# Conformer/RG-LRU block on one core: squares of the opening norm shared by two engines, and a gate operation moved ahead of convolution taps

## The chip, the cores and the metric

One core of a Trainium2 chip runs the whole program. The metric is the device time of one execution in microseconds (us); the kernel before took 876.96 us (median of 3 runs, 875.38 to 878.05). The core has five engines that work side by side and wait for each other through semaphores: TensorE (PE in the profile, its weight loads PEld), VectorE (DVE), ScalarE (ACT), GpSimd (POOL) and SyncE (SP), whose queue issues the DMAs here. [...]

## The reference, cut to what matters

One layer over 512 latent tokens and 256 context tokens, 1024 channels, all in fp32.

```python
hl = modulate(rmsnorm(x, g_pre_mix), sh1, sc1)        # sh, sc from silu(c) @ w_ada + b_ada
hc = modulate(rmsnorm(ctx, g_pre_mix), csh1, csc1)
glu, xr, gt, mg = split(hl @ w_in)                    # the context needs xr alone
u   = dwconv31(v * sigmoid(g))                        # Conformer branch, then LayerNorm, silu, projection
xr  = dwconv4(xr) + b
for d in (forward, backward):
    r = sigmoid(xr @ w_r[d] + b_r[d]);  i = sigmoid(xr @ w_i[d] + b_i[d])
    a = exp(-8 * r * softplus(-lam[d]));  u = sqrt(1 - a*a) * i * xr
    h_t = a_t * h_(t-1) + u_t                         # scan; the latents start from the context's last state
y  = (sigmoid(ga) * yA + sigmoid(gb) * ((sum of h) * gelu(gt)) @ w_lru) @ w_out
x  = x + gt1 * rmsnorm(y)
x  = x + gt2 * rmsnorm(conv_ffn(modulate(rmsnorm(x)), 3x3))
```

## The kernel before, in words

Activations lie with channels on the 128 partitions (8 blocks `b` of 128 channels) and tokens along the free dimension. Every matrix product is made of three fp32r matmuls (L134 to L136): a value is split into a high part (ACT copies it to fp32r) and a low part (a subtraction). For weights that is the pair L122 (ACT, `whi`) and L123 (`wlo`, mostly POOL, for some blocks DVE), called ahead of their use by `cvt_to`; for activations it is `split` (L138 to L140). So PE needs ACT and POOL behind every 128x1024 block of weights.

**The beginning** (L349 to L439). The four 128-token blocks of `x` are loaded; `norm_a` squares each on ACT with a running sum (L227), takes the root on ACT (L149), its reciprocal (L151) and the scaling (L230) on DVE. `norm_b` transposes the scaled blocks on PE and copies them out, half on DVE and half on ACT (L239, L241). Meanwhile `ada_mm(0)` makes the first shift and scale columns. `ada_h(q)` then modulates two channel blocks (`h`, L293, on DVE) and splits them into `Ahi` and `Alo`. The first matmuls of the program's main products (`firsts`, L378) wait for these.

**The loop over channel blocks** (L667 to L731, `b` = 1 to 8) does four things at a time: PE makes `xr`, `v`, `g`, `gt` products of blocks ahead and the four gate products of block b-1 (`gate_mm`); ACT does tanh, exp and the roots; DVE does the width-4 convolution (`xr_post`, L569 to L576), the gate operations `r_dve` (L613), `i_dve` (L617), the product `scans_mul` (L630, its second direction on POOL) and the scans of block b-2 (L636 to L638). PSUM gives the products of `xr` and of the gates two 1024-wide buffers in turn, so the next `xr` product must wait until `r_dve(b-1, 1)` has read its gate.

**The taps.** The width-31 depthwise convolution (`conv31`, L505) is a generator of DVE instructions: 244 of them, two blocks at a time, called taps here. `fill(n)` places the next n taps at that point of DVE's program. In the loop before, iterations 1 to 7 place 4 + 4 + 2 + 3 + 3 = 16 taps and iteration 8 places 8 + 6 + 3 + 3 = 20, 132 in all. The other 112 follow behind the loop (L775 to L790), beside the products `gb` and `yb`, 15 for each block. When they are done, POOL adds up the last blocks (`lnsum`, L533) and PE makes the LayerNorm's mean (`mean`, L814).

**Between loop and taps** DVE multiplies by the gelu branch and splits (`gt_post`, L660 and L140, tile `rgl`). ACT's `ga_act` (L763) reuses memory and waits for the last of these; behind it on ACT stand two tap products handed to ACT and POOL (`offload`, L545, L547), the gates `tg` and weight conversions, behind those on POOL the conversions `wlo` of the next weights.

The order of the work is written out by hand: there is no scheduler.

Of the kernel before, what the change touches and what calls it, by code (L numbers as in the profile page):

```python
# [8 lines left out]
F32 = mybir.dt.float32  # L9
F32R = mybir.dt.float32r  # L10
AF = mybir.ActivationFunctionType
ALU = mybir.AluOpType
PSUM = bass.MemoryType.PSUM

D = 1024
NB = 8
T = 512
TC = 256
TA = T + TC
# [4 lines left out]
EPS = 1e-6  # L24
# [13 lines left out]
def backbone_kernel(es: ExitStack, tc: tile.TileContext, x, ctxt, par, wadq, wada, win, wgate, wpc, wpl, wout,  # L38
                    wup, wdn, out):
    nc = tc.nc  # L40
    V, S, G, PE = nc.vector, nc.scalar, nc.gpsimd, nc.tensor
# [5 lines left out]
    st = es.enter_context(tc.tile_pool(name="st", bufs=4))  # L47
# [17 lines left out]
    ones = const.tile([128, 128], F32, name="ones")  # L65
# [3 lines left out]
    def flat(t):  # L69
        return t.rearrange("p a b -> p (a b)") if len(t.shape) == 3 else t  # L70

    def mm2(name):
        return ps_mm.tile([128, 1024], F32, tag="mm2", name=name)
# [88 lines left out]
    xs = pg.tile([128, 4, D], F32, tag="g", name="xs")  # L162
    xnT = pd.tile([128, NB, T], F32, tag="d", name="xnT")
    Ahi = pa.tile([128, NB, T], F32R, name="Ahi")
    Alo = pa.tile([128, NB, T], F32R, name="Alo")
# [57 lines left out]
    def norm_a(src_rows, slot, junk):  # L223
        if src_rows is not None:
            nc.sync.dma_start(out=slot, in_=src_rows)
        ss = st.tile([128, 1], F32, tag="ss", name="ss")
        S.activation(out=junk, in_=slot if len(junk.shape) == 2 else slot.rearrange("p (a b) -> p a b", b=junk.shape[2]),  # L227
                     func=AF.Square, accum_out=ss)
        r = rstd_of(ss, "x")
        V.tensor_scalar(out=slot, in0=slot, scalar1=r, scalar2=None, op0=ALU.mult)  # L230
# [14 lines left out]
    for v, nm in ((0, "c"), (1, "c_ctx")):  # L245
        S.activation(out=sT[:, :, v:v + 1], in_=col(nm).unsqueeze(2), func=AF.Silu)


    adl = const.tile([128, 48], F32, name="adl")
    adc = const.tile([128, 16], F32, name="adc")  # L250
    ggb = const.tile([128, D], F32, name="ggb")
    gsl = const.tile([128, 8], F32, name="gsl")
# [3 lines left out]
    def ada_load(q):  # L256
        for k2 in range(4):
            wq[q, k2] = pq.tile([128, 2, 512], F32, tag="wa", bufs=10, name="wa")
            nc.sync.dma_start(out=wq[q, k2], in_=wadq[q, :, 2 * k2:2 * k2 + 2, :])
# [19 lines left out]
    def ada_h(q):  # L279
        big, R = adp[q]  # L280
        tp = big[:, 128:256]
        PE.transpose(tp, R[:, 0:128], idn)
        tv = tp.rearrange("p (m j v) -> p m j v", m=2, j=2)
        for v, dst, gs in ((0, adl, gsl), (1, adc, gsc)):
            V.tensor_add(dst[:, 0:16].rearrange("p (m b) -> p m b", m=2)[:, :, 2 * q:2 * q + 2], tv[:, :, :, v],
                         col("b_ada", 0, 16).rearrange("p (m b) -> p m b", m=2)[:, :, 2 * q:2 * q + 2])
            V.scalar_tensor_tensor(out=gs[:, 2 * q:2 * q + 2], in0=dst[:, 8 + 2 * q:10 + 2 * q], scalar=1.0,
                                   in1=col("g_pre_mix", 2 * q, 2), op0=ALU.add, op1=ALU.mult)
            if v == 0:
                hs = []  # L290
                for k in (2 * q, 2 * q + 1):
                    h = t_tile("h")
                    V.tensor_scalar(out=h, in0=xnT[:, k, :], scalar1=gsl[:, k:k + 1], scalar2=adl[:, k:k + 1],  # L293
                                    op0=ALU.mult, op1=ALU.add)
                    hs.append(h)
                for k, h in zip((2 * q, 2 * q + 1), hs):
                    split(h, Ahi[:, k, :], Alo[:, k, :])
# [46 lines left out]
    def warm(ps, n):  # L344
        for _ in range(n):
            PE.matmul(ps[:, 0:128], ones, ones, start=True, stop=True)

    psA, psC = mm2("xr_ps"), mm2("vg_ps")
    for t in range(4):  # L349
        norm_a(x[128 * t:128 * t + 128, :], xs[:, t, :], flat(Alo[:, 2 * t:2 * t + 2, :]))  # L350
    ada_load(0)
    warm(psA, 20)
    for t in range(4):
        norm_b(xs[:, t, :], xnT[:, :, 128 * t:128 * t + 128])
# [87 lines left out]
    pre = st.tile([128, 1], F32, tag="sd", name="pre")  # L442
# [107 lines left out]
    rec = pd.tile([128, NB, T], F32, tag="d", name="rec")  # L550
    filler = conv31()

    def fill(n):
        for _ in range(n):
            if not next(filler, False):
                return
# [75 lines left out]
    def scans(b):  # L632
        (a0, _), (a1, _) = lru[b, 0], lru[b, 1]
        u0, u1 = lru[b, 0, 1], lru[b, 1, 1]
        hc = pl.tile([128, TC], F32, tag="hc", name="hc")
        V.tensor_tensor_scan(hc, a0[:, T:TA], u0[:, T:TA], 0.0, ALU.mult, ALU.add)  # L636
        V.tensor_tensor_scan(rec[:, b, :], a0[:, 0:T], u0[:, 0:T], hc[:, TC - 1:TC], ALU.mult, ALU.add)  # L637
        V.tensor_tensor_scan(u1[:, TA - 1::-1], a1[:, TA - 1::-1], u1[:, TA - 1::-1], 0.0, ALU.mult, ALU.add)  # L638
        (V if b == 7 else G).tensor_add(rec[:, b, :], rec[:, b, :], u1[:, 0:T])

# [26 lines left out]
    for b in range(1, NB + 1):  # L667
        last = b == NB
        if last:
            gt_block(3)  # L670
            gt_copy(3)
        else:
            w = W(("xr", b))
            if b == 1:
                ps = ps1
            else:
                ps = mm2("xr_ps")
                block(ps[:, 0:T], w, Ahi, Alo)
        if b >= 2:
            scans_act(b - 2)  # L680
        if not last:
            block(ps[:, T:T + TP], w, chi, clo)
        fill(8 if last else 4)
        if b >= 2:
            scans_mul(b - 2)
        W(("gate", b - 1))
        gate_mm(b - 1, 0, 0)
        if not last:
            xw = xr_act(b, ps)
        r_act(b - 1, 0)  # L690
        if b + 1 < NB:
            psv = mm1("v_ps")
            block(psv, W(("v", b + 1)), Ahi, Alo)
        else:
            gt_block(1 if b < NB else 4)
            gt_copy(1 if b < NB else 4)
        fill(0 if last else 4)
        if not last:
            xr_post(b, ps, xw, 0)
            xc_new = xcs.pop(b)  # L700
        r_dve(b - 1, 0)
        if b >= 2:
            scans(b - 2)
        fill(6 if last else 2)
        gate_mm(b - 1, 0, 1)
        if last:
            gt_block(5)
        gate_mm(b - 1, 1, 0)
        gate_tanh(b - 1, 0, 1)
        r_act(b - 1, 1)  # L710
        i_dve(b - 1, 0)
        if b + 1 < NB:
            glu_mul(tg, psv, b + 1)
        if b + 2 < NB:
            psg = mm1("g_ps")
            block(psg, W(("g", b + 2)), Ahi, Alo)
        else:
            gt_block((0, 2, 6)[b - 6])
            if not last:
                gt_copy((0, 2)[b - 6])  # L720
        fill(3)
        r_dve(b - 1, 1)
        fill(3)
        gate_mm(b - 1, 1, 1)
        gate_tanh(b - 1, 1, 1)
        if not last:
            xcs[b] = xc_new
            xc_split(b)
        if b + 2 < NB:
            tg = gate_act(psg)  # L730
        i_dve(b - 1, 1)  # L731
# [509 lines left out]
```

## Time and profile before

| what | value |
|---|---|
| median of 3 runs | 876.96 us (875.38 to 878.05) |
| the profiled execution's own time | 875.37 us |
| its span in the trace | 873.6 us |
| PE busy | 851.4 us (97%) |
| DVE busy | 662.5 us (76%) |
| ACT busy | 432.5 us (50%) |
| POOL busy | 410.7 us (47%) |
| mean granted TensorE clock | 0.996 |

The span is what the trace's times count; 1.8 us of the execution lie around it. "Busy" is a mean over stages: the strip of 40 slices on the page shows PE at 7 tenths in the first slice and 9 in all others but the last, and DVE at 3 to 5 tenths in the first four, at 9 from the sixth to the seventeenth, and at 3 to 5 for some slices after the eighteenth. A matmul's record is longer than its share of the engine, because matmuls overlap: a 128x512 one is 0.39 us long and the next starts 0.23 us after it.

### The profile page before, as it was taken

What the parts mean: (1) busy time and instruction counts of PE and PEld (TensorE: products, weight loads), DVE (VectorE), ACT (ScalarE), POOL (GpSimd) and SP (SyncE); (2) the same over time, 40 slices, a digit from 0 to 9 for tenths busy, and PEclk for the clock granted to TensorE, in tenths of its full rate; (3) what the DMA queues carried; (4) which work ended last, traced back from release to release, by engine and by line L of the source; (5) the groups of instructions that cost most, each with busy time, mean ns of one, the idle gap of its engine ahead of it and who ended that gap; (6) DMA issues with size and microseconds to landing.
All of it is one profiled execution on the core that took longest, in us unless ns stands there. A gap on an engine that the chain in (4) does not pass through costs nothing.

```text
span 873.6 us, 11376 instructions
## 1 busy us (share of the span) xinstructions
PE 851.4 (97%) x4312; PEld 690.1 (79%) x4312; DVE 662.5 (76%) x929; ACT 432.5 (50%) x614; POOL 410.7 (47%) x227
## 2 busy tenths in 40 slices
PE   7999999999999999999999999999999999999997
PEld 6777877887787878887688889888888888888785
DVE  4355899999998999973555254999998998989204
ACT  5283776686767542225743355544443444345222
POOL 1234554555555665464232313545655456457720
PEclk9999999999999999999999999999999999999999
DMA  9952122121222232252843411224333333324402
GB/s 352 385 210 85 62 83 75 66 79 61 85 73 96 73 111 83 97 192 95 339 145 121 179 39 50 97 96 136 118 121 108 121 120 107 115 94 134 156 0 97
DMA packets 31398, 106.01 MB, mean 121 GB/s; under 512 B 3440, under 2 KB 3568, under 8 KB 31344
## 3 DMA queue, kind: packets, MB, share of 16 engines
q1 hardware_dynamic: 31344, 105.29, 34.4%
q8 instruction: 34, 0.56, 0.3%
q14 instruction: 20, 0.16, 0.1%
HBM read 103.17 MB, written 2.10 MB: 121 GB/s over the span
## 4 chain that ended last, share of the span: by engine, by line
PE 79%; DVE 11%; ACT 5%; issue 3%; DMA 0%; POOL 0%; DVEq 0%; SPq 0%; ACTq 0%; POOLq 0%
PE up_ps L135 9%; PE up_ps L136 9%; PE up_ps L134 9%; PE xr_ps L134 3%; DVE rec L637 3%; PE xr_ps L135 3%; PE xr_ps L136 2%; DVE cv L521 2%; PE ya_ps L134 2%; PE y_ps L135 2%; PE ya_ps L136 2%; PE y_ps L134 2%; PE ya_ps L135 2%; PE y_ps L136 2%; PE yb_ps L134 1%
## 5 line engine op out<-in xcount | busy, mean ns | idle before, releaser
L123 POOL TENSOR_TENSOR wlo<-raw,whi 128x1024 fp32r<-128x1024 f32 x117 | 291.8, 2507 | 232.9 <-ACT whi L122 232.7
L1035 DVE SCALAR_TENSOR_TENSOR cv<-zall,P,cv 128x512 f32<-128x512 f32 x240 | 161.8, 743 | 0.2
L521 DVE SCALAR_TENSOR_TENSOR cv<-glu,P,cv 128x512 f32<-128x512 f32 x228 | 153.8, 740 | 0.0
L122 ACT ACTIVATE whi<-raw 128x1024 fp32r<-128x1024 f32 x121 | 125.2, 1053 | 22.5 <-issue 8.0
L134 PE MATMUL up_ps<-Ahi,whi 128*128 128x512 f32 (+1 forms) x352 | 131.8, 375 | 0.0
L136 PE MATMUL up_ps<-Ahi,wlo 128*128 128x512 f32 (+1 forms) x352 | 131.7, 374 | 0.0
L135 PE MATMUL up_ps<-Alo,whi 128*128 128x512 f32 (+1 forms) x352 | 131.6, 374 | 0.0
L135 PEld LDWEIGHTS up_ps<-Alo,whi 128*128 128x128 f32 x352 | 66.0, 188 | 13.2
L136 PEld LDWEIGHTS up_ps<-Ahi,wlo 128*128 128x128 f32 x352 | 66.0, 188 | 13.3
L134 PEld LDWEIGHTS up_ps<-Ahi,whi 128*128 128x128 f32 x352 | 66.0, 188 | 13.1
L1021 POOL TENSOR_TENSOR acl<-fo,ach 128x512 fp32r<-128x512 f32 x20 | 26.0, 1300 | 85.5 <-ACT ach L1018 85.5
L1035 DVE SCALAR_TENSOR_TENSOR cv<-zall,P,cc 128x512 f32<-128x512 f32 x40 | 43.2, 1108 | 21.2 <-ACT cc L1009 21.2
L1007 ACT ACTIVATE zall<-up_ps 128x512 f32<-128x512 f32 x40 | 23.7, 593 | 63.5 <-PE up_ps L136 63.5
L1018 ACT ACTIVATE ach<-fo 128x512 fp32r<-128x512 f32 x20 | 12.7, 633 | 66.8 <-DVE fo L1017 66.8
L598 ACT ACTIVATE gate_ps<-gate_ps,P 128x768 f32<-128x768 f32 x32 | 28.0, 875 | 34.2 <-PE gate_ps L136 33.7
L134 PE MATMUL xr_ps<-Ahi,whi 128*128 128x512 f32 x56 | 22.6, 404 | 6.9 <-DVE e L613 6.9
L364 ACT ACTIVATE tg<-gb_ps 128x512 f32<-128x512 f32 x8 | 4.8, 596 | 48.9 <-PE gb_ps L136 48.9
L1009 ACT ACTIVATE cc<-up_ps,P 128x512 f32<-128x512 f32 x40 | 27.3, 682 | 1.9 <-DVE cv L1035 1.9
L1035 DVE SCALAR_TENSOR_TENSOR fo<-zall,P,cv 128x512 f32<-128x512 f32 x40 | 27.9, 734 | 0.0
L140 POOL TENSOR_TENSOR xl<-xc,xh 128x768 fp32r<-128x768 f32 x8 | 14.9, 1859 | 27.5 <-ACT xh L139 27.5
L134 PE MATMUL gt_ps<-Ahi,whi 128*128 128x512 f32 x64 | 26.0, 407 | 1.5 <-DVE e L613 1.5
L136 PE MATMUL gt_ps<-Ahi,wlo 128*128 128x512 f32 x64 | 25.9, 404 | 0.3 <-POOL wlo L123 0.3
(380 smaller groups left out, 2120.9 us busy)
## 6 DMA issues: line engine op xcount, KB each, us to landing
raw<-in_win_dram SPq DMA_DIRECT2D x48, 512.0 KB, 3.3
raw<-in_wup_dram SPq DMA_DIRECT2D x40, 512.0 KB, 3.3
wa<-in_wada_dram SPq DMA_DIRECT2D x24, 512.0 KB, 5.7
raw<-in_wdn_dram SPq DMA_DIRECT2D x22, 512.0 KB, 3.4
wa<-in_wadq_dram SPq DMA_DIRECT2D x16, 512.0 KB, 9.1
raw<-in_wpl_dram SPq DMA_DIRECT2D x8, 512.0 KB, 3.3
raw<-in_wpc_dram SPq DMA_DIRECT2D x8, 512.0 KB, 4.8
raw<-in_wout_dram SPq DMA_DIRECT2D x8, 512.0 KB, 3.3
```

The source lines that it names most:

```text
L122: S.activation(out=flat(hl[0]), in_=flat(t), func=AF.Copy)
L123: eng.tensor_sub(flat(hl[1]), flat(t), flat(hl[0]))
L134: PE.matmul(o, lh, rh, start=first, stop=False)
L135: PE.matmul(o, lh, rl, start=False, stop=False)
L136: PE.matmul(o, ll, rh, start=False, stop=last)
L521: V.scalar_tensor_tensor(out=cv[b] if k else glu[:, b, 0:T], in0=glu[:, b, k:k + T], scalar=col("dw31", 31 * b + k, 1), in1=cv[b], op0=ALU ...
L598: S.activation(out=lru[b, d, q], in_=lru[b, d, q], func=AF.Tanh, scale=0.5, bias=hb[:, i:i + 1])
L637: V.tensor_tensor_scan(rec[:, b, :], a0[:, 0:T], u0[:, 0:T], hc[:, TC - 1:TC], ALU.mult, ALU.add)
L1007: S.activation(out=z[:, 1:1 + GH, 1:1 + GW], in_=ps.rearrange("p (r c) -> p r c", c=GW), func=AF.Copy)
L1009: S.activation(out=c, in_=ps.rearrange("p (r c) -> p r c", c=GW), func=AF.Copy, scale=col("dw9", 9 * (i + FW * (1 - s)) + 4, 1))
L1021: G.tensor_sub(acl[:, i, :], fo[i, 0], ach[:, i, :])
L1035: V.scalar_tensor_tensor(out=o, in0=zz[i, s][:, k // 3:k // 3 + GH, k % 3:k % 3 + GW], scalar=col("dw9", 9 * (i + FW * (1 - s)) + k, 1), i ...
```

## The change

- Beginning: ACT squares blocks 0 and 2 of `x`, DVE (as a product of the block with itself, with a running sum) blocks 1 and 3. The root's function table is loaded by a one-column root (`pre`) ahead of the first square. Sums and roots lie in two tiles of four columns.
- `ada_h(0)`: the first of its two modulated blocks is made by ACT (`Identity` with scale and bias), the second by DVE as before.
- Loop: `r_dve(b-1, 1)` stands ahead of the taps that stood before it. The taps of iterations 2 to 7 fall from 16 to 14, those of iteration 8 from 20 to 19; iteration 1 keeps 16. That makes 119 taps in the loop and 125 behind it.
- Scans: the context's scan writes over its input `u0` instead of a tile `hc`, and the latents' scan starts from that column.

```diff
@@ before the start
+    pre = st.tile([128, 1], F32, tag="sd", name="pre")
+    S.activation(out=pre, in_=ones[:, 0:1], func=AF.Sqrt)
@@ ada_h
-                    V.tensor_scalar(out=h, in0=xnT[:, k, :], scalar1=gsl[:, k:k + 1], scalar2=adl[:, k:k + 1],
-                                    op0=ALU.mult, op1=ALU.add)
+                    if k:
+                        V.tensor_scalar(out=h, in0=xnT[:, k, :], scalar1=gsl[:, k:k + 1], scalar2=adl[:, k:k + 1],
+                                        op0=ALU.mult, op1=ALU.add)
+                    else:
+                        S.activation(out=h, in_=xnT[:, k, :], func=AF.Identity, scale=gsl[:, k:k + 1],
+                                     bias=adl[:, k:k + 1])
@@ the opening norm
+    ss4, sd4 = [st.tile([128, 4], F32, tag="n4" + n, bufs=1, name="n4" + n) for n in "sd"]
     for t in range(4):
-        norm_a(x[128 * t:128 * t + 128, :], xs[:, t, :], flat(Alo[:, 2 * t:2 * t + 2, :]))
+        nc.sync.dma_start(out=xs[:, t, :], in_=x[128 * t:128 * t + 128, :])
     ada_load(0)
+    for t in (1, 0, 3, 2):
+        junk = flat(Alo[:, 2 * t:2 * t + 2, :])
+        if t % 2:
+            V.scalar_tensor_tensor(out=junk, in0=xs[:, t, :], scalar=1.0, in1=xs[:, t, :], op0=ALU.mult, op1=ALU.mult,
+                                   accum_out=ss4[:, t:t + 1])
+            continue
+        S.activation(out=junk, in_=xs[:, t, :], func=AF.Square, accum_out=ss4[:, t:t + 1])
+        for i in (t, t + 1):
+            S.activation(out=sd4[:, i:i + 1], in_=ss4[:, i:i + 1], func=AF.Sqrt, scale=1.0 / D, bias=EPS)
+            V.reciprocal(sd4[:, i:i + 1], sd4[:, i:i + 1])
+            V.tensor_scalar(out=xs[:, i, :], in0=xs[:, i, :], scalar1=sd4[:, i:i + 1], scalar2=None, op0=ALU.mult)
@@ scans
-        hc = pl.tile([128, TC], F32, tag="hc", name="hc")
-        V.tensor_tensor_scan(hc, a0[:, T:TA], u0[:, T:TA], 0.0, ALU.mult, ALU.add)
-        V.tensor_tensor_scan(rec[:, b, :], a0[:, 0:T], u0[:, 0:T], hc[:, TC - 1:TC], ALU.mult, ALU.add)
+        V.tensor_tensor_scan(u0[:, T:TA], a0[:, T:TA], u0[:, T:TA], 0.0, ALU.mult, ALU.add)
+        V.tensor_tensor_scan(rec[:, b, :], a0[:, 0:T], u0[:, 0:T], u0[:, TA - 1:TA], ALU.mult, ALU.add)
@@ the loop over b
-        fill(0 if last else 4)
+        fill(0 if last else 4 if b == 1 else 3)
...
-        fill(3)
         r_dve(b - 1, 1)
-        fill(3)
+        fill(6 if b == 1 else 5)
```

The loop on DVE, iteration 2, from the context's scan to `i_dve(1, 1)`; `e` is the decay factor that `r_dve` works on, `cv` and `glu` are the taps' tiles, `u` is `i_dve`'s result. Before:

```order
L636 SCALAR_TENSOR_TENSOR hc<-a,u 128x256
L637 SCALAR_TENSOR_TENSOR rec<-a,hc,u 128x512
L638 SCALAR_TENSOR_TENSOR u<-a,u 128x768
...
L368 SCALAR_TENSOR_TENSOR glu<-tg,v_ps 128x512
L521 SCALAR_TENSOR_TENSOR cv_921<-glu,P,cv_921 128x512
L521 SCALAR_TENSOR_TENSOR cv_923<-glu,P,cv_923 128x512
L521 SCALAR_TENSOR_TENSOR cv_921<-glu,P,cv_921 128x512
L613 SCALAR_TENSOR_TENSOR e_1221<-e_1221,gate_ps 128x768
```

And now:

```order
L655 SCALAR_TENSOR_TENSOR u<-a,u 128x256
L656 SCALAR_TENSOR_TENSOR rec<-a,u 128x512
L657 SCALAR_TENSOR_TENSOR u<-a,u 128x768
...
L388 SCALAR_TENSOR_TENSOR glu<-tg,v_ps 128x512
L633 SCALAR_TENSOR_TENSOR e_1211<-e_1211,gate_ps 128x768
L541 SCALAR_TENSOR_TENSOR cv_915<-glu,P,cv_915 128x512
L541 SCALAR_TENSOR_TENSOR cv_913<-glu,P,cv_913 128x512
L541 SCALAR_TENSOR_TENSOR cv_915<-glu,P,cv_915 128x512
```

The gate operation (L613, now L633) stands directly behind the `glu` product, and five taps follow it before `i_dve` where three stood ahead and three behind.

DVE at the beginning, from its first instruction to the copies of the transposed blocks; `n4s` and `n4d` are the sums and roots. Before:

```order
L151 RECIPROCAL rsx<-sdx 128x1
L230 TENSOR_SCALAR xs<-xs,rsx 128x1024
...
L241 COPY xnT<-tp_ps 128x4x128 x4
L277 COPY R<-ada_ps 128x128
L285 TENSOR_TENSOR adl<-ada_ps,P 128x2x2
L287 SCALAR_TENSOR_TENSOR gsl<-adl,P 128x2
L293 TENSOR_SCALAR h<-xnT,gsl,adl 128x512 x2
L140 TENSOR_TENSOR Alo<-h,Ahi 128x512 x2
```

And now:

```order
L364 SCALAR_TENSOR_TENSOR Alo,n4s<-xs 128x1024
L370 RECIPROCAL n4d<-n4d 128x1
L371 TENSOR_SCALAR xs<-xs,n4d 128x1024
...
L241 COPY xnT<-tp_ps 128x4x128 x4
L280 COPY R<-ada_ps 128x128
L288 TENSOR_TENSOR adl<-ada_ps,P 128x2x2
L290 SCALAR_TENSOR_TENSOR gsl<-adl,P 128x2
L297 TENSOR_SCALAR h<-xnT,gsl,adl 128x512
L140 TENSOR_TENSOR Alo<-h,Ahi 128x512 x2
```

DVE has two squares more ahead of the copies (the second stands in the rows left out, between the second and the third scaling) and one modulation less.

## Rows read from the trace of the kernel before

**Rows 1.** Waits of PE, 110 to 260 us and 260 to 320: total, times, longest.
```profile
PE xr_ps L134 <- DVE e L613: 6.9, 5, 1.4
...
PE gt_ps L134 <- DVE e L613: 1.5, 1, 1.5
```

**Rows 2.** Windows: length, busy us of each engine, granted clock, DMA share, GB/s.
```profile
134.30:159.90 25.60, 24.23 (x122) 20.16 (x122) 25.25 (x30) 18.71 (x23) 13.89 (x7) 1.00 0.22 73
...
280.00:282.00 2.00, 1.93 (x5) 1.54 (x6) 2.00 (x5) 1.99 (x3) 0.00 (x0) 0.55 0.71 221
282.00:284.00 2.00, 2.00 (x7) 1.57 (x6) 2.00 (x4) 1.98 (x3) 0.60 (x1) 0.60 0.11 43
```

**Rows 3.** Timeline of DVE in one loop iteration: start us, length us, instruction.
```profile
147.02 2.06 DVE L521 SCALAR_TENSOR_TENSOR cv<-glu,P,cv 128x512 f32<-128x512 f32 x3
149.00 0.94 DVE L613 SCALAR_TENSOR_TENSOR e<-e,gate_ps 128x768 f32<-128x768 f32 x1
...
155.33 2.02 DVE L630 TENSOR_TENSOR u<-u,e 128x768 f32<-128x768 f32 x1
```

**Rows 4.** Timeline of PE in the same iteration.
```profile
148.34 0.28 PE L136 MATMUL gate_ps<-xh,gwl 128*128 128x256 f32 x1
149.99 0.50 PE L134 MATMUL xr_ps<-Ahi,whi 128*128 128x512 f32 x1 [1.37 <-DVE e L613]
```

**Rows 5.** Timeline of POOL in the same iteration.
```profile
154.69 1.85 POOL L630 TENSOR_TENSOR u<-u,e 128x768 f32<-128x768 f32 x1
```

**Rows 6.** The chain of waits, 296 to 320 us: start us, length us, piece.
```profile
314.48 1.50 POOL wlo L123
...
316.03 0.50 PE gb_ps L136
```

**Rows 7.** Timeline of DVE: the first taps behind the loop.
```profile
307.86 13.25 DVE L521 SCALAR_TENSOR_TENSOR cv<-glu,P,cv 128x512 f32<-128x512 f32 x20
```

**Rows 8.** Timeline of POOL: the last sums for the mean.
```profile
385.36 2.47 POOL L533 TENSOR_TENSOR lnsum<-lnsum,glu 128x512 f32<-128x512 f32 x2 [1.47 <-DVE glu L521]
```

**Rows 9.** Timeline of PE: the mean.
```profile
396.82 1.02 PE L814 MATMUL mean<-lnsum,ones 128*128 128x512 f32 x2
```

**Rows 10.** The scans' lines: count, shortest/median/longest ns, first and last start.
```profile
L637 DVE TENSOR_TENSOR_SCAN rec<-a,hc,u x8: 3232/3235/3248, 113.9 to 285.2; 128x512 f32<-128x512 f32 x8
...
L638 DVE TENSOR_TENSOR_SCAN u<-a,u x8: 1725/1726/1727, 117.1 to 288.4; 128x768 f32<-128x768 f32 x8
```

**Rows 11.** Timeline of ACT at the beginning.
```profile
4.84 1.06 ACT L227 ACTIVATE Alo<-xs 128x1024 fp32r<-128x1024 f32 x1 [0.45 <-DMA xs<-in_x_dram]
5.80 0.19 ACT L227 ACTIVATION_READ_ACCUMULATOR Alo<-xs 128x1 f32 x1
6.00 1.28 ACT L149 ACT_TABLE_LOAD   x1
7.30 0.20 ACT L149 ACTIVATE sdx<-ss 128x1 f32<-128x1 f32 x1
```

**Rows 12.** Timeline of SP: weight loads that wait for blocks 0 and 1 of x.
```profile
5.22 1.21 SPq L105 DMA_DIRECT2D raw<-in_win_dram  x2
```

**Rows 13.** Timeline of DVE at the beginning.
```profile
11.35 0.17 DVE L151 RECIPROCAL rsx<-sdx 128x1 f32<-128x1 f32 x1 [0.32 <-ACT sdx L149]
11.55 0.76 DVE L230 TENSOR_SCALAR xs<-xs,rsx 128x1024 f32<-128x1024 f32 x1
...
18.56 3.00 DVE L293 TENSOR_SCALAR h<-xnT,gsl,adl 128x512 f32<-128x512 f32 x2
21.80 1.29 DVE L140 TENSOR_TENSOR Alo<-h,Ahi 128x512 fp32r<-128x512 f32 x2 [0.24 <-ACT Ahi L139]
```

**Rows 14.** Timeline of POOL at the beginning.
```profile
18.48 2.35 POOL L123 TENSOR_TENSOR w0l<-raw,w0h 128x1024 fp32r<-128x1024 f32 x1 [1.26 <-ACT w0h L122]
```

**Rows 15.** Groups by line and form of DVE and of ACT: busy us, mean ns.
```profile
L931 DVE SCALAR_TENSOR_TENSOR x<-xw,rsy,x 128x1024 f32<-128x1024 f32 x4 | 5.1, 1285 | 0.1
...
L857 ACT ACTIVATE glu<-glu,P 128x512 f32<-128x512 f32 x8 | 6.4, 805 | 1.9 <-DVE glu L856 1.9
```

## The prediction, made before the run

> **What bounds the kernel now.** I read the table of busy shares first: PE is busy 97% of the span, so little is to be had except where PE stands still, and a change off PE's path counts only through PE's waits. So the second view is PE's waits by releaser. From 110 to 260 us one line holds all of them: five waits of the `xr` product on DVE's gate operation, 6.9 us together, the longest 1.4; behind 260 us the same operation holds `gt` up once, for 1.5 us [rows 1]. The third view is the windows: one iteration of the loop, 25.60 us, has PE busy 24.23 and DVE busy 25.25 [rows 2]. There DVE is the bound, and PE loses the difference, 1.37 us. The fourth is the timeline of one iteration. DVE works off three taps from 147.02, then the gate operation from 149.00 for 0.94 [rows 3]; PE's last gate matmul starts at 148.34 and the next product only at 149.99, behind a wait of 1.37 [rows 4]. A tap costs (149.00 - 147.02) / 3 = 0.66 us; the record of the three ends at 149.08, so DVE's instructions overlap by 0.08.
>
> **The change, part by part.**
>
> *Gate operation ahead of the taps.* It needs nothing from them. It would start at 147.02 and end at 147.96. PE's last gate matmul starts at 148.34 and lasts 0.28, so PE itself is ready at about 148.5: 0.5 us later. The wait goes, in iterations 2 to 6.
>
> *Two taps fewer per iteration.* Reordering alone would only move the wait, since DVE's work per iteration (25.25) exceeds PE's (24.23). Less 2 x 0.66 it is 23.93, and PE is the bound, by 0.3 us. What is late next is DVE's multiplication L630: it starts at 155.33 and takes 2.02 [rows 3], because POOL's own half runs from 154.69 to 156.54 [rows 5]; it ends about 0.8 us behind POOL's end, however early it starts. With one tap ahead of it gone the gain there is lost, and only the tap behind it shortens the way to the next gate operation. By my count this uses up nearly all of the 0.5 us. I take 6.8 of the 6.9 us; the bounds are 3.4 (half of each wait stays) and 6.9.
>
> *Behind the loop.* Iteration 8 has one tap less between its gate operation and the end of `gt_post`: DVE is there 0.66 earlier. [...] But the chain of waits shows what is next: POOL's `wlo` at 314.48 releases PE's `gb` at 316.03 [rows 6]. That chain hangs on DVE: `gt_post` ends as the taps begin at 307.86 [rows 7], ACT and POOL follow. [...] Only 0.66 is kept. A wait longer than the one of 1.5 probably costs the clock again: I take 1.6 us back; bounds 0 and 1.7.
>
> *125 taps behind the loop for 112.* From 307.86, 20 taps take 13.25 [rows 7], 0.66 each; 13 more are 8.6 us. POOL's last sums ended at 385.36 + 2.47 = 387.83 [rows 8], the mean started at 396.82 [rows 9]: 9.0 us of room. DVE starts the taps earlier by 6.8 + 0.66 and PE reaches the mean earlier by the same less the clock's 1.6, so the room shrinks to about 9.0 - 8.6 + 1.6 = 2.0 us. Cost nothing, by this cover; if it is gone, the mean waits for every further 0.1 us.
>
> *Scan in place.* The 256-column scan writes where it reads. The backward scan does so already: 768 columns in 1.726 us [rows 10]. The latents' scan, not in place and started from a column, takes 3.235 for 512 [rows 10], which by the other's rate would be 1.15; something adds 2.1. Value 0; bounds: +2.1 per iteration if the in-place scan is hit too, -2.1 if the start column in `hc` was the reason.
>
> *Squares and root table.* ACT's load of the root's table, 1.28 us, stood between the first square and its root at 7.30 [rows 11]. ACT had been idle for 0.45 when block 0 came at 4.84 [rows 11]; the load now starts in that gap, at 4.39, and ends at 5.67, so the first square starts 0.9 later than before and its root comes only some 0.3 earlier. Block 1 had landed by 6.43, when the issue that waits for it ended [rows 12]. From there DVE does, one behind the other, square 1, two reciprocals and scalings, square 3, and again two of each. A square is nearest to L931, 1.285 [rows 15], a reciprocal with its scaling 0.2 + 0.76 [rows 13]: 6.43 + 2 x 1.285 + 3 x 0.96 + 0.2 = 12.1 for the last scaling's start, against 11.55 [rows 13]; with an overlap of 0.08 for each of the eight steps 11.4. A sum's readout, 0.19 on ACT [rows 11], may come twice on top. So -0.9 to +0.15; I take 0.
>
> *Modulated block on ACT.* DVE's two modulations took 3.00 us [rows 13], where the first ran into POOL's subtraction of 18.48 to 20.83 [rows 14] and ended behind it. Now DVE's single one meets the same, and ends near 21.1; but block 0 is made and split on ACT by then (0.81 [rows 15] and a copy), and its low part can start at about 21.1 instead of 21.80 [rows 13]. That is 0.7 for PE; behind it the weights' conversions follow 0.5 to 0.7 earlier. I take 0.5. [...]
>
> *Sum.* 0.5 + 6.8 + 0.66 - 1.6 = 6.4 us. Against the profiled execution's own 875.37 (span 873.6 and 1.8 around it) that is 869.0. That execution lies 1.6 under the median of the runs, 876.96; against the median I forecast **870.6**.
>
> **The rivals.**
> - *The clock stays up* at the new wait, as it did behind the waits of 1.37. Then nothing is given back: 869.0. For it: only one wait in these rows is followed by the low clock. Against: the new wait is longer than that one.
> - *DVE stays late.* L630 keeps ending behind POOL, and half of each wait remains: 3.4 us less gain, 874.0. For it: the count above leaves under 0.1 us.
> - *The start loses.* Both readouts come and the scalings end 0.9 later, so that the start gives -0.4 instead of +0.5: 871.5. [...]
> - *The taps only move.* If they run 2% slower there, or DVE idles, the 2.0 us of room at the mean are gone, and in the end all 8.6 come back as a wait there: at most no gain but the start's, 876.5.
> - *Slower:* the in-place scan pays the 2.1 us that the latents' scan pays [rows 10]. DVE's iteration is 23.93 + 2.1 = 26.0, 0.4 more than 25.60: five iterations 2.1, and two more such scans lie in the chain behind iteration 8, 4.2. With 0.5 and 0.66 off: 876.96 + 5.1 = 882. It decides from some 1.7 us per scan on. Against it: the backward scan is in place at the ordinary rate.
>
> **How the numbers follow.** Forecast 0.50 (869.5 to 872), clock up 0.16, start loses 0.08, DVE late 0.12, taps only move 0.08, slower 0.06. A measurement of this kernel can tell about 0.3% from no change, 2.6 us, so below 874.3 is faster: the first four, 0.86. No change 0.08, slower 0.06. The range is 867.9 to 873.9: below, the clock case with the start's and the runs' spread of about 1 us; above, nearly the case of DVE late. The last two cases are left out.
>
> **What would show it.** Right: PE's waits on the gate operation gone from 110 to 260 us, iterations near 24.2 us, PE busy for all of one; a wait of PE on `wlo` near 308 us of some 2.5 us, with a granted clock near 0.5 behind it; the mean not waiting for `lnsum`; the 256-column scan near 0.68. Wrong: iterations above 24.6 us, a wait before the mean, or a scan above 2 us; the last would turn the sign.

## The result and the profile after

The changed kernel took 867.16 us (median of 4 runs, 866.13 to 869.42) beside 876.65 us for the kernel before (4 runs): a ratio of 0.9895, 95% interval 0.987 to 0.992, or 9.5 us less. The forecast was 870.6 with a range of 867.9 to 873.9: the sign was right, and the gain was half as large again as the 6.4 us that were worked out. The profiled execution of the changed kernel took 866.80, its span is 865.0 for 873.6 before, 8.6 us less.

PE's waits from 110 to 260 us and from 260 to 330 us, where those of [rows 1] stood (line, releaser, total us, times, longest):

```profile
PE gt_ps L136 <- POOL wlo L123: 0.3, 1, 0.3
...
PE yb_ps L134 <- ACT sa L781: 1.7, 1, 1.7
PE gb_ps L136 <- POOL wlo L123: 1.0, 1, 1.0
PE gt_ps L136 <- POOL wlo L123: 0.3, 1, 0.3
PE gate_ps L134 <- DVE u L637: 0.2, 1, 0.2
```

The waits on the gate operation are gone, all six. Two others have come behind the loop, 1.7 us (on `sa`, which ACT's `ga_act` writes) and 1.0. One iteration in the windows, and the four microseconds behind the first of the new waits, against [rows 2] (length, busy us of PE, PEld, DVE, ACT, POOL, granted clock, DMA share, GB/s):

```profile
131.30:155.24 23.94, 23.94 (x122) 20.12 (x121) 22.88 (x28) 18.66 (x23) 14.54 (x8) 1.00 0.24 78
...
300.00:302.00 2.00, 1.94 (x8) 1.62 (x9) 2.00 (x4) 2.00 (x5) 0.00 (x0) 1.00 0.00 0
302.00:304.00 2.00, 2.00 (x10) 1.62 (x9) 2.00 (x4) 2.00 (x4) 1.60 (x2) 1.00 0.00 0
```

PE is busy for all of the iteration. DVE's busy time fell from 25.25 to 22.88, by 2.37 and not by the 1.32 of two taps. And the clock stayed at 1.00 behind the wait of 1.7.

PE's timeline shows what a wait had cost (start us, length us, instruction); it answers to [rows 4]:

```profile
146.48 0.28 PE L135 MATMUL gate_ps<-xl,gwh 128*128 128x256 f32 x1
146.60 0.29 PE L136 MATMUL gate_ps<-xh,gwl 128*128 128x256 f32 x1
146.72 0.39 PE L134 MATMUL xr_ps<-Ahi,whi 128*128 128x512 f32 x1
146.95 0.39 PE L135 MATMUL xr_ps<-Alo,whi 128*128 128x512 f32 x1
```

The product begins 0.12 us behind the start of the last gate matmul. Before it began 149.99 - 148.34 = 1.65 behind it, 1.53 later, though the wait is listed as 1.37: that figure is counted from the matmul's recorded end (0.28 long), and without a wait the next one would have begun before that end. Then the first matmul after the stop is slower: in the trace before its follower starts 0.34 behind it (149.99 to 150.33), here 0.23.

```profile
150.33 0.39 PE L135 MATMUL xr_ps<-Alo,whi 128*128 128x512 f32 x1
```

Together 1.64. PE's lead, that is how much earlier a matmul starts than the same one in the trace before, agrees: at the starts of the `xr` products it is 0.17 us (99 us of the trace before), 1.68, 3.27, 4.87, 6.49 and 8.10 (227 us), so 1.6 a wait.

DVE and POOL in the same iteration, against [rows 3, 5]:

```profile
145.25 0.94 DVE L633 SCALAR_TENSOR_TENSOR e<-e,gate_ps 128x768 f32<-128x768 f32 x1
146.12 3.38 DVE L541 SCALAR_TENSOR_TENSOR cv<-glu,P,cv 128x512 f32<-128x512 f32 x5
...
152.91 0.94 DVE L650 TENSOR_TENSOR u<-u,e 128x768 f32<-128x768 f32 x1
```

```profile
137.09 2.75 POOL L123 TENSOR_TENSOR wlo<-raw,whi 128x1024 fp32r<-128x1024 f32 x1 [3.10 <-ACT whi L122]
...
152.96 2.61 POOL L650 TENSOR_TENSOR u<-u,e 128x768 f32<-128x768 f32 x1
```

DVE's multiplication now begins 0.05 ahead of POOL's half and takes 0.94 for 2.02; POOL's half, which ran its 1.85 undisturbed before, takes 2.61. In both traces the one that started first ran at its usual length, and the other stood.

Behind the loop, DVE and POOL (DVE first); this is the chain that ends in the two new waits:

```profile
276.39 3.25 DVE L656 TENSOR_TENSOR_SCAN rec<-a,u 128x512 f32<-128x512 f32 x1
279.56 1.73 DVE L657 TENSOR_TENSOR_SCAN u<-a,u 128x768 f32<-128x768 f32 x1
...
281.93 10.43 DVE L679 TENSOR_TENSOR ge<-ge,rec 128x512 f32<-128x512 f32 x8
292.29 7.01 DVE L140 TENSOR_TENSOR rgl<-ge,rgh 128x512 fp32r<-128x512 f32 x6
```

```profile
275.20 3.35 POOL L123 TENSOR_TENSOR wlo<-raw,whi 128x1024 fp32r<-128x1024 f32 x1 [4.91 <-ACT whi L122]
281.63 5.47 POOL L123 TENSOR_TENSOR wlo<-raw,whi 128x1024 fp32r<-128x1024 f32 x2 [3.08 <-PE ga_ps L136]
```

The scan that [rows 10] had at 3.235 is 3.25 here. POOL's operation beside it ends at 275.20 + 3.35 = 278.55, and the scan at 279.64, 1.09 later, though it had started at 276.39. In the iterations it is the same: POOL ends at 137.09 + 2.75 = 139.84, the scan (137.68, 3.24 long) at 140.92, 1.08 later. That gives a reason for the 2.1 us that the prediction could not name: a wait for POOL, and not the column that the scan starts from. The experiments below test it.

At the mean, POOL and PE, against [rows 8, 9]:

```profile
385.27 2.46 POOL L553 TENSOR_TENSOR lnsum<-lnsum,glu 128x512 f32<-128x512 f32 x2 [7.62 <-DVE glu L541]
```

```profile
388.22 1.02 PE L832 MATMUL mean<-lnsum,ones 128*128 128x512 f32 x2
```

The last sums end at 387.73, 0.5 us ahead of the mean: the 13 taps are still hidden, with 0.5 to spare for 9.0 before.

The beginning, on ACT, DVE and PE, against [rows 11, 13]:

```profile
4.52 1.28 ACT L249 ACT_TABLE_LOAD   x1
5.82 0.20 ACT L249 ACTIVATE pre<-ones 128x1 f32<-128x1 f32 x1
...
18.82 0.81 ACT L300 ACTIVATE h<-xnT,adl,gsl 128x512 f32<-128x512 f32 x1 [0.17 <-DVE gsl L290]
```

```profile
9.61 1.23 DVE L364 SCALAR_TENSOR_TENSOR Alo<-xs 128x1024 fp32r<-128x1024 f32 x1 [0.29 <-DMA xs<-in_x_dram]
...
11.81 0.75 DVE L371 TENSOR_SCALAR xs<-xs,n4d 128x1024 f32<-128x1024 f32 x1
...
18.82 2.56 DVE L297 TENSOR_SCALAR h<-xnT,gsl,adl 128x512 f32<-128x512 f32 x1
```

```profile
22.04 0.50 PE L135 MATMUL xr_ps<-Alo,w0h 128*128 128x512 f32 x1 [1.20 <-DVE Alo L140]
```

In the trace before:

```profile
22.55 0.50 PE L135 MATMUL xr_ps<-Alo,w0h 128*128 128x512 f32 x1 [0.23 <-DVE Alo L140]
```

The last scaling starts at 11.81, 0.26 later than before, since its square waits for block 3 to land at 9.61. From there to the first low part 0.77 is won, so that one comes 0.51 earlier. PE then waits 0.28 us for DVE's next conversion, which starts at 23.03 for 23.28, and is 0.26 ahead at 28 us. When the blocks land differs from execution to execution: over all profiles of this case the last scaling starts at 11.35 to 11.81 with the new start (eight profiles, median 11.54) and at 11.55 to 12.31 with the old (five, median 11.82). So the 0.26 is that of one pair of executions.

### The profile page after: what moved, and what is told of

Same layout as the page of the kernel before. It is cut to its first block, busy times and chain, and to the rows that moved or that the text cites. A ratio compares the mean times of both kernels' runs of the same rounds, so it can differ in the third digit from the quotient of the medians.

```text
span 865.0 us, 11373 instructions
## 1 busy us (share of the span) xinstructions
PE 848.0 (98%) x4312; PEld 688.6 (80%) x4312; DVE 659.8 (76%) x932; ACT 431.5 (50%) x612; POOL 411.6 (48%) x227
## 4 chain that ended last, share of the span: by engine, by line
PE 88%; DVE 6%; ACT 3%; issue 1%; DMA 1%; POOL 0%; SPq 0%; DVEq 0%; ACTq 0%; POOLq 0%
PE up_ps L135 9%; PE up_ps L134 9%; PE up_ps L136 9%; PE xr_ps L135 3%; PE xr_ps L136 3%; PE xr_ps L134 2%; PE ya_ps L134 2%; PE y_ps L134 2%; PE y_ps L135 2%; PE ya_ps L135 2%; PE ya_ps L136 2%; PE y_ps L136 2%; PE yb_ps L136 2%; PE yb_ps L135 2%; PE yb_ps L134 2%; PE g_ps L136 1%
## 5 line engine op out<-in xcount | busy, mean ns | idle before, releaser
L134 PEld LDWEIGHTS up_ps<-Ahi,whi 128*128 128x128 f32 x352 | 66.1, 188 | 13.7
L134 PE MATMUL yb_ps<-rgh,whi 128*128 128x512 f32 x64 | 25.4, 396 | 1.7 <-ACT sa L781 1.7
L136 PE MATMUL gb_ps<-Ahi,wlo 128*128 128x512 f32 x64 | 25.3, 395 | 1.0 <-POOL wlo L123 1.0
L134 PE MATMUL ga_ps<-Ahi,whi 128*128 128x512 f32 x64 | 26.0, 406 | 0.0
```

Of the source, the lines that this page charges most:

```text
L134: PE.matmul(o, lh, rh, start=first, stop=False)
L136: PE.matmul(o, ll, rh, start=False, stop=last)
```

## The experiments

Every kernel was timed beside the kernel before on the same chip; the ratio is to that, with its 95% interval.

**The loop's part alone** (the kernel before with this edit):

```diff
-        fill(0 if last else 4)
+        fill(0 if last else 4 if b == 1 else 3)
...
-        fill(3)
         r_dve(b - 1, 1)
-        fill(3)
+        fill(6 if b == 1 else 5)
```

> The kernel before with the loop's part alone (gate operation ahead of its taps, 14 taps for 16, 13 taps more behind the loop); start and scans as before. Theory A (the whole gain is the loop's and what follows from it): iterations of 23.95 us as in the changed kernel, 0.2 us behind the changed kernel, so about 867.4. Theory B (the part of the gain above the forecast came from the start or the scans in place): 1.5 to 3 us behind the changed kernel, 868.7 to 870.2.

868.6 us (5 runs, 867.68 to 870.77), ratio 0.9917 (0.9905 to 0.993). The loop is as expected: iterations of 23.9 us and both new waits, 1.7 and 1.0. The median lies 1.4 us behind the changed kernel's, which would speak for theory B. The profiled execution, 869.77, shows where its part of this arose: it was 2.8 us behind the kernel before at the first `g` product (26.61 for 23.82), in a stretch where the two programs are the same. Its windows there:

```profile
14.00:16.00 2.00, 2.00 (x22) 1.58 (x21) 0.00 (x0) 0.57 (x1) 0.00 (x0) 0.50 1.00 410
24.00:26.00 2.00, 1.79 (x5) 1.41 (x5) 1.97 (x5) 1.95 (x3) 0.00 (x0) 0.50 1.02 410
```

The granted clock was at 0.50 where the kernel before had 1.00 in both windows. So what this pair of times says of the start is mixed with the clock. Behind the start the trace decides for theory A: from the `xr` product at 99 us to the mean, PE's lead grows by 8.7 us (from -2.78 to 5.88), in the changed kernel by 8.4 (0.17 to 8.60). The loop's part is the whole gain there, and what the start adds is left to the next run.

**The start's part alone** (squares by turns, the table ahead, one block on ACT, as in the change's diff; loop and scans as before).

> The kernel before with the start's part alone (squares by turns, root's table ahead, one modulated block on ACT). Theory A: the trace of the changed kernel has PE 0.2 us ahead from 30 us on, so 0.2 us less than before, 876.4 to 876.8, no change that can be told. Theory B (the start brought the rest): 874 to 875. The five waits of 1.37 us on the gate operation stay in both.

875.55 us (11 runs), ratio 0.9995 (0.9985 to 1.0005): no difference that can be told, theory A; the interval leaves room for a gain of up to 1.3 us. PE's five waits stand at 6.7 us together. PE's lead at 28 us is 0.66 in this profile, at the full clock, and not 0.26.

**The order without the taps**: 16 taps stay in each iteration.

```diff
-        fill(3)
         r_dve(b - 1, 1)
-        fill(3)
+        fill(6)
```

> The kernel before with the gate operation ahead of its taps, and all 16 taps kept in each iteration. Theory A (DVE's work of 25.2 us per iteration is then the bound, since its multiplication still starts behind POOL's half and takes 2.0 us): iterations of 25.2 to 25.3 us, a wait of PE somewhere else in each, 1.5 to 2 us less than before, about 875. Theory B (the order alone does it; the multiplication gets ahead of POOL's half and takes 0.94): iterations of about 24.2 us, 6 to 7 us less than before, about 870.

869.56 us (5 runs), ratio 0.9923 (0.9909 to 0.9937): 6.6 us of gain, theory B, and not my theory A. One iteration of it in the windows, then DVE's operations that had stood behind POOL:

```profile
132.00:156.00 24.00, 24.00 (x122) 20.14 (x121) 23.89 (x30) 18.75 (x24) 13.63 (x8) 1.00 0.22 78
```

```profile
155.69 1.58 DVE L630 TENSOR_TENSOR u<-u,e 128x768 f32<-128x768 f32 x1
...
163.85 1.90 DVE L636 TENSOR_TENSOR_SCAN hc<-a,u 128x256 f32<-128x256 f32 x1
165.79 1.28 DVE L637 TENSOR_TENSOR_SCAN rec<-a,hc,u 128x512 f32<-128x512 f32 x1
```

The two scans in the kernel before:

```profile
138.74 0.69 DVE L636 TENSOR_TENSOR_SCAN hc<-a,u 128x256 f32<-128x256 f32 x1
139.46 3.23 DVE L637 TENSOR_TENSOR_SCAN rec<-a,hc,u 128x512 f32<-128x512 f32 x1
```

With all 16 taps DVE is busy for 23.89 and no longer for 25.25. Of the 1.36 less, 0.44 are at the multiplication (1.58 for 2.02) and 0.74 at the two scans (3.18 for 0.69 + 3.23). The 25.25 was not DVE's work but its work and what it stood behind POOL; when PE's stall went, the two engines met elsewhere, and that part shrank. PE is the bound by 0.1 us. By PE's lead the order alone wins 7.8 us in the loop (-1.53 to 6.25), against 8.1 for the loop's whole part (-2.78 to 5.36). What is not hidden stands behind the loop: a wait of 2.2 us on `sa`, with the clock at 0.50 behind it (304 to 306 us).

**The taps without the order**: 14 taps for 16 in iterations 2 to 7, the gate operation behind three of them as before.

```diff
-        fill(0 if last else 4)
+        fill(0 if last else 4 if b == 1 else 3)
...
         fill(3)
         r_dve(b - 1, 1)
-        fill(3)
+        fill(3 if b == 1 else 2)
```

> The kernel before with 14 taps for 16 in iterations 2 to 7 and the gate operation where it was, behind three taps. Theory A (the stall hangs on the place of the gate operation, not on the sum of DVE's work): its end stays about 16.7 us behind the end of the xr product, so PE's five waits stay near 1.4 us each, iterations 25.4 to 25.6 us, no change that can be told, about 876.5. Theory B (the sum of DVE's work is the bound): iterations of about 24.2 us and 869 to 871.

875.46 us (11 runs), ratio 0.9997 (0.9988 to 1.0006): theory A, nothing. PE's waits on the gate operation, 110 to 260 us and behind, then DVE's wait at the head of one iteration's convolution:

```profile
PE xr_ps L134 <- DVE e L613: 6.9, 5, 1.4
PE gt_ps L134 <- DVE e L613: 1.5, 1, 1.5
```

```profile
134.46 1.02 DVE L569 SCALAR_TENSOR_TENSOR xw<-xr_ps,P,xw 128x770 f32<-128x770 f32 x1 [2.26 <-ACT xw L563]
```

Two taps fewer leave each wait as long as it was. The time that they free becomes DVE's idle time: behind PE's `xr` product ACT makes the convolution's first term (`xw`), DVE waits 2.26 us for it and goes on from there to the gate operation, and three taps stood on that way. So the order is the change. What the moved taps add to it can't be told from the times (0.9917 with them, 0.9923 without); by PE's lead from 99 us to the mean it is 1.2 us (8.7 for 7.5), 0.4 of it in the loop and the rest behind it, where the wait on `sa` is 2.2 for 1.7 and the clock is at 0.73 and then 0.50 (302 to 306 us), for 1.00 in the changed kernel.

**The scans in place alone** (the kernel before with the change's two lines on them).

> The kernel before with the scans in place alone. Theory A: the 256-element scan 0.68, the 512-element scan 3.24 as before, no change that can be told, 875.5 to 877. Theory B (the start column's own tile cost the 512-element scan its 2 us, or the in-place scan is slower): 512-element scans under 2 us, or 256-element scans over 2 us, and 3 us less or more.

876.49 us (10 runs), ratio 1.0005 (0.9995 to 1.0014). The 512-element scans take 3.233 us in the median, the 256-element ones 0.684: theory A.

**The changed kernel again**, for the clock.

> The changed kernel once more, to have it on the same chip as the three below, and for the clock behind PE's new wait of 1.7 us near 299 us. Theory A (a wait longer than the 1.5 us of the kernel before brings the clock down, as the prediction had it): granted clock 0.5 to 0.6 for some 4 us behind 300 us, and 1.4 to 1.7 us lost there. Theory B (the same wait brings it down in some executions and not in others; the first profile of the changed kernel had 1.00 there): 1.00 again in this profile or not, with no rule by its length. Time 866 to 869.

866.92 us (6 runs, 866.14 to 869.94), ratio 0.9895 (0.9875 to 0.9915). The wait of 1.7 is there, and the clock behind it is 1.00 once more: theory A falls. The start came out better in this execution, with block 3 there at 9.17:

```profile
9.17 1.23 DVE L364 SCALAR_TENSOR_TENSOR Alo<-xs 128x1024 fp32r<-128x1024 f32 x1 [0.17 <-DMA xs<-in_x_dram]
...
11.37 0.75 DVE L371 TENSOR_SCALAR xs<-xs,n4d 128x1024 f32<-128x1024 f32 x1
```

PE's lead at 28 us is 0.70 here. For the clock, the profiles set side by side have:

```
wait            profiles in which the clock fell behind it, and those in which it did not
1.5 (gt_ps)     fell: before, start alone       stayed: taps alone, scans alone
1.7 (yb_ps)     fell: none                      stayed: changed (twice), loop alone, first weight on DVE
2.2 (yb_ps)     fell: order alone
```

Behind the wait of 1.5 the clock was at 0.55 in the kernel before and at 0.50 in the start alone (280 to 282 us), and at 1.00 in the other two: the same wait at the same place, with the fall behind it in some executions and not in others. What decides it stays open.

**A quiet POOL beside the last scans.** In the changed kernel one weight's low part, which POOL makes beside them, is made by DVE ahead of them:

```diff
-        queue(("ga", b), win[32 + b], wb)
+        queue(("ga", b), win[32 + b], wb, eng=V if b else G)
...
     scans_mul(7)
+    cvt_to(index["ga", 1])
     scans(7)
```

(`gt_block(7)` converts one weight fewer ahead.)

> The changed kernel with one weight's low part (the second ga weight), which POOL makes beside the last iteration's scans, made on DVE ahead of them; the scan still starts from a column. Theory A (the 512-element scan stands until POOL's operation beside it has ended): the last such scan takes 1.1 to 1.3 us and not 3.25, DVE pays 1.23 for the conversion, its chain ends 0.8 us earlier, PE's wait of 1.7 near 299 us shrinks to about 0.9. Theory B (starting from a column costs 2.1 us): the scan stays at 3.25, DVE's chain ends 1.2 us later and PE's wait grows to about 2.9.

```profile
275.20 1.21 DVE L123 TENSOR_TENSOR wlo<-raw,whi 128x1024 fp32r<-128x1024 f32 x1
276.34 0.68 DVE L655 TENSOR_TENSOR_SCAN u<-a,u 128x256 f32<-128x256 f32 x1
277.05 1.28 DVE L656 TENSOR_TENSOR_SCAN rec<-a,u 128x512 f32<-128x512 f32 x1
```

Theory A: with the same start column and without POOL the scan takes 1.28, and PE's wait on `sa` is 0.9. In time it can't be told from the changed kernel: 867.45 (5 runs), ratio 0.9891 (0.9871 to 0.9911). At the scan (1.28 for 3.25) and at the multiplication above (0.94 for 2.02, and POOL's half 2.61 for 1.85) it was the operation that had started second that took longer. What the two engines share there no run shows.

**The same for the whole stretch behind the loop**: four weights' low parts and all of the split products on DVE.

```diff
-    queue(("gb", 0), win[40], wb)
+    queue(("gb", 0), win[40], wb, eng=V)
...
-            queue(("gb", b + 1), win[41 + b], wb)
-        queue(("yb", b), wpl[b], wb)
+            queue(("gb", b + 1), win[41 + b], wb, eng=G if b else V)
+        queue(("yb", b), wpl[b], wb, eng=G if b else V)
...
-            split(gts[b], rgh[:, b, :], rgl[:, b, :], G if b % 3 == 2 else V)
+            split(gts[b], rgh[:, b, :], rgl[:, b, :], V)
...
```

(with the edit above, `gb` 0 made behind five multiplications, `gb` 1 and `yb` 0 behind the splits; the lines that move them are left out)

> The changed kernel with POOL kept idle behind the last iteration until the products of the scans are split: the low parts of four weights (ga 1, gb 0, gb 1, yb 0) and of two product blocks made on DVE. Theory A (DVE's multiplications and subtractions there, 1.2 to 1.3 us each, stand behind POOL's for half of their time): each takes 0.6 to 0.7, DVE reaches the taps at 294 to 296 us and not at 299.2, both of PE's waits (1.7 and 1.0) go, 2.5 to 2.9 us less than the changed kernel on this chip. Theory B (the operations take 1.2 on DVE anyway): DVE gains nothing and has four conversions more, 4.9 us, so PE's wait grows and the time with it, 3 to 5 us more.

```profile
282.46 3.09 DVE L679 TENSOR_TENSOR ge<-ge,rec 128x512 f32<-128x512 f32 x5
285.47 1.22 DVE L123 TENSOR_TENSOR wlo<-raw,whi 128x1024 fp32r<-128x1024 f32 x1
286.60 1.89 DVE L679 TENSOR_TENSOR ge<-ge,rec 128x512 f32<-128x512 f32 x3
288.41 4.90 DVE L140 TENSOR_TENSOR rgl<-ge,rgh 128x512 fp32r<-128x512 f32 x8
```

POOL stands idle for 24.74 us meanwhile:

```profile
296.40 2.56 POOL L567 TENSOR_TENSOR off_acc<-off_acc,off_prod 128x512 f32<-128x512 f32 x2 [24.74 <-ACT off_prod L565]
```

Theory A: a multiplication takes 0.6 for 1.3, a subtraction 0.6 for 1.2. DVE has more to do, four conversions and two subtractions, and reaches the taps at 295.5 for 299.2, though this execution was 1.4 us late from the start (clock at 0.50 there). Both of PE's waits are gone. 865.18 us (5 runs), ratio 0.9866 (0.9846 to 0.9887): 1.7 us under the changed kernel on the same chip, of the 2.5 to 2.9 expected, and with intervals that overlap. Why it is less than expected stays open.

**The first weight's low part on DVE**, ahead of its modulated block:

```diff
-    queue(("xr", 0), win[16], wb, lambda: (w0h, w0l))
+    queue(("xr", 0), win[16], wb, lambda: (w0h, w0l), eng=V)
...
             if v == 0:
+                cvt_to(0)
                 hs = []
...
-    cvt_to(0)
     ada_h(0)
```

> The changed kernel with the low part of the first weight, POOL's from 18.73 to 21.10, made on DVE, ahead of DVE's one modulated block. Theory A (that block, 2.56 us, stands behind POOL): the block takes about 0.6, the conversion 1.23, PE's wait of 1.2 us near 21 us shrinks to 0.5, and 0.3 to 0.7 us of it are kept at 30 us. Theory B (what PE gains there it waits for later at the start, on the transfers of the modulation's weights): nothing is kept at 60 us.

```profile
19.72 1.23 DVE L123 TENSOR_TENSOR w0l<-raw,w0h 128x1024 fp32r<-128x1024 f32 x1
20.86 0.54 DVE L298 TENSOR_SCALAR h<-xnT,gsl,adl 128x512 f32<-128x512 f32 x1
```

The block takes 0.54 for 2.56, and PE's wait of 1.2 is 0.2. This execution had a granted clock of 0.64 and 0.51 at 12 to 16 us and was 1.0 late from there, so it was level with the changed kernel at 23 us; the time is 866.86 (6 runs), ratio 0.9885 (0.9866 to 0.9904), not to be told from it. The next run, at a clock of 1.00 there, shows the gain kept.

**Both together**, and **both with 12 dummy products** of 128 columns on PE in the gaps of the start:

```diff
         norm_b(xs[:, t, :], xnT[:, :, 128 * t:128 * t + 128])
+        if t == 0:
+            warm(psC, 8)
         ada_mm(0, (t,))
+        if t == 0:
+            warm(psC, 4)
```

> The changed kernel with both edits: POOL idle behind the last iteration (as in the run before it) and the first weight's low part on DVE. Theory A (the two places are apart and their gains add): no wait of PE between 260 and 330 us, PE's first wait for a subtracted block 0.2 us and not 1.2, 0.5 to 0.9 us less than with the first edit alone where the clock at the start is the same: 864 to 865, the fastest runs near 863. Theory B (the start's gain is taken by a later wait): 865.2 as with the first edit alone.

> The same with 12 more dummy products of 128 columns on PE, 8 and 4, in the stretches from 9.7 to 13.2 us in which PE stood still. Theory A (the clock's falls at 12 to 18 us and 22 to 28 us in some executions come after PE has stood there): granted clock 1.00 from 10 to 30 us in the profile, the runs lie within 2 us of each other and not within 3.7, median 863 to 864. Theory B (the falls come by chance whatever PE does there, or the added products delay the transposes): the spread stays, and the median with it or up to 0.5 us more.

Both together: 863.8 us (4 runs, 863.27 to 866.14), ratio 0.9863 (0.9848 to 0.9878), a little better than expected; the first `g` product starts at 22.39 for 23.40 in the first profile of the changed kernel (the last scaling starts at 11.81 in both), and the 1.0 us is still there at 27 us. With the dummy products: 862.92 us (4 runs, 862.28 to 863.66), ratio 0.985 (0.9833 to 0.9866), 13.7 us less than the kernel before and below the changed kernel's interval. The windows of the last one at the start:

```profile
14.00:16.00 2.00, 2.00 (x41) 1.44 (x32) 0.71 (x2) 1.00 (x2) 0.00 (x0) 1.00 1.02 410
24.00:26.00 2.00, 2.00 (x62) 1.63 (x65) 0.00 (x0) 0.00 (x0) 1.43 (x1) 1.00 1.01 404
```

The clock is at 1.00, where the loop alone had 0.50, and the four runs lie within 1.4 us, for 2.9 without the dummies; their mean granted clocks are 0.998 to 0.999, for 0.995 to 0.999. That fits theory A, but four runs are few, and among the seven other profiles with the new start the clock at the start had also stayed up in five (1.00 from 10 to 30 us in the changed kernel's first and in that of both together). So it is not shown.

## Why the prediction was wrong in size

Two terms of the sum were mis-sized, the loop and the clock, and two steps of the reasoning were false. By the steps, with PE's lead over the trace before as the measure:

- **The start, +0.5 predicted, +0.26 at 28 us** (0.17 at 99 us) in this pair of profiles, and 0.66 to 0.71 in three others with the new start at the full clock (the changed kernel again, the start alone, the quiet POOL). The modulated block on ACT won 0.77 for PE's first low part (11.81 to 22.04 for 11.55 to 22.55), of which PE's wait for DVE's next conversion left about 0.5, as forecast. The squares cost 0.26 in this pair where I took 0, inside the bounds of -0.9 and +0.15; over all profiles the last scaling starts 0.28 earlier in the median. I let DVE's chain start at block 1's landing and did not ask when block 3 lands, and that varies (its square starts at 9.61 in one execution of the changed kernel and at 9.17 in the other). DVE's readouts of its sums took 0.08 each and hid, and the operation behind the table load starts 0.02 after its end (4.52 + 1.28 = 5.80, and 5.82). So the rival "the start loses" fell. Beside POOL's operation DVE took 2.56 for a block and ACT 0.81; with POOL out of the way DVE took 0.54. So of the two engines ACT was the faster for this block only beside POOL's operation.
- **The loop, +6.8 predicted, +8.0 measured** (lead 0.17 to 8.22). The first term that was mis-sized. The step "I take 6.8 of the 6.9 us; the bounds are 3.4 and 6.9" took the listed idle time for the price of the wait. The price was 1.6 a wait and not 1.37: the overlap of two matmuls that a stop takes away (0.16) and the slow first matmul behind it (0.11) come on top, so the upper bound was too low.
- **"Reordering alone would only move the wait, since DVE's work per iteration (25.25) exceeds PE's (24.23)"** failed, and this is the mechanism and not a size. The order alone gave 6.6 us, the taps alone nothing; the 25.25 held DVE's standing behind POOL. So did "it ends about 0.8 us behind POOL's end, however early it starts": DVE's multiplication started 0.05 ahead of POOL's and ran free. These two steps did not cost the sum much, and that was luck: I counted both edits together and came out at nearly the whole wait. They would have misled anyone who had to choose between them.
- **Behind the loop, +0.66 predicted, +0.5 measured.** PE won 3.3 there (lead 8.19 to 9.86 as the wait of 1.5 went, to 11.52 by the clock, which stayed at 1.00) and gave back 2.9, in two waits (lead 11.53 to 9.67 at `yb`, to 8.66 at `gb`) and not in one of some 2.5. The step named `wlo` alone; ACT's `sa`, which waits for the same `rgl`, comes first.
- **The clock, -1.6 predicted, 0 measured.** The second term that failed: "a wait longer than the one of 1.5 probably costs the clock again". It was built on one wait in one execution [rows 1, 2]. No run shows the 1.6 behind the changed kernel's new waits: in four profiles of four the clock stayed at 1.00 behind the one of 1.7. My rival "the clock stays up", with 0.16, was what happened.
- **13 taps behind the loop and the scans in place, 0 each**: right. The room at the mean is 0.5 us; I had 2.0 with the clock's 1.6 in it, so 0.4 without; that the taps stayed hidden hung on half a microsecond.

The sum: 0.2 + 8.0 + 0.5 is the lead of 8.7 at 313 us, and 8.6 is left at the end. The 1.2 of the loop and the 1.6 of the clock, less 0.3 at the start and 0.2 behind the loop, are the 2.3 us between 6.4 and 8.7. The medians lie 9.5 apart, since the profiled execution of before was 1.3 under its median and that of after 0.4; the cause of these 0.9 stays open.

## What to carry to other kernels

Price a removed wait by the starts of the instructions around it, with and without the wait, and not by its listed idle time (1.6 us for 1.37 here). An engine's busy share can hold time in which it stood behind another engine's operation (25.25 us an iteration here, and 23.89 with the same taps when it stood less), so take the fastest run of the same operation elsewhere as its work, before calling the engine the bound. And where a small operation that others wait for stands behind filler, move the operation first (ratio 0.9923 here); taking filler away that did not stand on the way to it brought nothing (0.9997).

## What the runs showed of the hardware that was not expected

- Some of DVE's operations took longer beside a POOL operation that had started first: a 512-element scan 3.25 us for 1.28, a 512-element multiplication 1.3 for 0.6, a subtraction 1.2 for 0.6, the modulated block 2.56 for 0.54. The taps did not: beside POOL 13 of them took 8.64 us from 303.83 on, 0.66 each as elsewhere. By the kernel's tiles the taps have an input in PSUM and the others have theirs in SBUF; whether that is the reason no run shows. It goes both ways: POOL's 768-element product took 2.61 for 1.85 when DVE was first. DVE alone made a 128x1024 low part in 1.2 us, POOL in 2.4; with four of them and two subtractions taken over from POOL behind the loop, DVE reached the taps at 295.5 for 299.2.
- A stop of PE cost more than its listed idle time: 1.6 us for 1.37, five times over.
- The granted clock fell behind a wait of 1.5 us in two profiles of four, to 0.55 and 0.50 in the 2 us behind it, and behind one of 2.2, to 0.50, in the only profile that had it. It did not behind one of 1.7 in four of four, nor behind the twenty waits of 1.3 to 1.4 in the loops of four profiles. At the start it fell, in the same instructions, in some executions and not in others: at 14 to 16 us it was 0.50 in the loop alone and 1.00 in the kernel before. In the profile of the loop alone PE was 2.8 us late behind two such falls; that is most of the difference between that profile and the changed kernel's (spans of 868.0 and 865.0 us).
